# Smaller pieces of the residual and gate loads, more load buffers and another product order in a mixture-of-experts block

## The chip, the cores and the metric

The kernel runs on one core of one Trainium2 chip. The metric is the device time of one launch in microseconds (us), the median of several runs. The engines are TensorE (PE in the rows; its weight loads are PEld), VectorE (DVE), ScalarE (ACT), GpSimd (POOL) and SyncE (SP). SyncE here only issues DMA transfers.

## The reference, cut to what matters

One layer of a transformer block over 256 tokens of width 2048: an attention and pooling part, then a feed-forward part with 16384 experts, of which every token picks 128 (8 heads, 16 each) with a gate. All of it is float32.

```python
mod = silu(c) @ ada_w + ada_b                      # 6 vectors of 2048
shift1, scale1, gate1, shift2, scale2, gate2 = split(mod, 6)
...                                                # attention and pooling part gives h
xn2 = rms_norm(h, norm2_g) * (1 + scale2) + shift2
# peer_ffn: router scores, top 16 of 16 x 16 candidates a head, softmax gates
a   = gelu(xn2 . w_down[expert]) * gate            # for the 128 chosen experts of a token
out = sum over the chosen experts of a * w_up[expert]
h   = h + gate2 * out
return rms_norm(h, final_g)
```

## The kernel before

**The order of the work.** The kernel is a list of steps that run one after the other. A step is one block of weights of 128 x 2048 float32 (1 MB), read as two halves of 128 x 1024 (0.5 MB), and the matmuls on it. The list holds the first projections, attention with its output, the router's queries, and then the expert part, which is computed densely for the first 192 tokens (`ND`): every one of the 128 blocks of 128 experts is multiplied with all 192 tokens, and a gate that is zero for experts not chosen is multiplied in between. The last 64 tokens (`SP`) are done sparsely: their chosen rows are gathered from memory and worked on by VectorE (`sparse_step`, 128 gathers of 1 MB, spread over the steps; 0.95, 0.47, 0.42 and 0.55 a step in the four stages below, the first of them from its step 24 on).

The expert part has four stages of 64 steps (`HB`): half 0 down, half 0 up, half 1 down, half 1 up. Both halves and both products are in `steps`; `n0` is the first down step of a half where the loop over `half` uses it, and after that loop it is the first down step of half 1. The text below counts the steps of each stage from 0.

**A step's matmuls.** In half 0 the down step is `exact`: float32 matmuls straight from the load buffer (`L353`, 16 products, each of which the trace shows as two matmuls). In the other steps each half of a block is split: ScalarE casts it to a rounded part `hi` (`L166`), VectorE subtracts that and leaves the rest `lo` (`L172`). There are 4 buffers of each (`HL_BUFS`). In half 1 down `pair` multiplies `hi` with both parts of the tokens (384 columns, `L189`) and `lo` with the rounded part (192 columns, `L190`). In the up steps the token side is stationary, and it is split too: `prep` casts on ScalarE (`L1114`) and subtracts twice on VectorE (`L1116`). The results stay in all 8 banks of PSUM for the 64 steps: bank `2q+t` holds column quarter `q` (512 columns) of token group `t`. Tokens 0 to 127 (`t = 0`) have a rounded and a rest part of 128 columns each (H and L below); tokens 128 to 191 (`t = 1`) have both parts side by side in one stationary operand of 128 columns (X), and `fold` adds the two halves of the result at the end. With `wh` and `wl` for the two parts of the weights a quarter needs H wh, L wh, H wl, X wh, X wl: five matmuls, twenty a step. A step calls `mm` twice (`part` 0 and 1), each for two quarters, that is, for one half of the block.

The order inside a part is all products with `hi` and then all with `lo`. In the last step of all the order is another (`last`): the eight X products first, `hi` and `lo` by turns.

**Loads.** `want` puts all loads of the kernel in one list in the order of their use. `fill` issues them on SyncE's queue as long as a buffer is free: 5 buffers `raw`, and behind them the list `spare`, which is filled with other memory for some stretches (`room(True)`: three pieces of `hT`, in half 0 up from step 1 to the last 8 steps, and again from step 26 of half 1 down). `take` gets the oldest load, `give` returns its buffer and calls `fill`. In half 0 down, steps 0 to 19 also carry the last 20 of the 32 halves of the modulation matrix for `gate2` (`ada_half`): VectorE multiplies the load with `cb` and sums it (`L219`), so one load in three waits for VectorE there. In the same steps VectorE runs the router's selection (`route`), in the order of the program.

**The three things around it.**
- `load_gates(q)` brings the gates of half 1 back from memory (`g2d`, written by half 0) into the tile that will take the activations: tiles 0 and 1 in half 0 up, tile 2 at step 0 of half 1 down, a small tile 3 at step 24. A tile is one transfer of 2 MB on SyncE's queue.
- At step 1 of half 1 down one transfer of 2 MB on SyncE's queue brings `hT` (the block's input, parked in `hsp`) back.
- `residual`, a generator that moves on twice a step, begins after step 4 of half 1 down: it finishes `gate2` on GpSimd (`ada_fix`), stores it as a row, loads it broadcast to all partitions (`g2b`), both on GpSimd's queue, which also issues the gathers; after four turns of rest it transposes `hT` on TensorE, four blocks at a time, and VectorE multiplies half 0's result with `g2b` and adds the transposed block (`L1231`, `L1232`), eight times.

`tick` is one function that a step may carry; it is called behind the step's matmuls, its row work and its side work.

Of the kernel before, what the change touches and what calls it, by code (L numbers as in the profile page):

```python
# [93 lines left out]
def peer_block_kernel(ctx: ExitStack, tc, xT_d, c_d, cols_d, const_d, ada_d, gates_d, wide_d, blk_d, mix_d, br_d,  # L94
# [151 lines left out]
    class Step:  # L246
        def __init__(self, src, mm, evac=None, w=D, ada=(), before=(), after=(), tick=None, exact=False):
            self.exact = exact
            self.src, self.mm, self.evac, self.w = src, mm, evac, w
            self.ada, self.before, self.after, self.tick = list(ada), list(before), list(after), tick  # L250
            self.hs, self.ls = [], []
            self.rows = 0
# [48 lines left out]
    def run():  # L301
# [11 lines left out]
        for n, parts in plan():  # L313
# [18 lines left out]
            if s:  # L332
                side_step(1)
                if s.tick:
                    s.tick()
# [467 lines left out]
    steps[w0 + 2].tick = lambda: table(AF.Sqrt)  # L803
# [211 lines left out]
    def load_gates(q):  # L1015

        a = get_A(half_state[1], q)
        nc.sync.dma_start(a, g2d[:, :, q * AB:q * AB + a.shape[2], :])
# [73 lines left out]

    def open_late():
# [10 lines left out]
    def up_step(half, bl, oc):  # L1104
# [15 lines left out]
        def mm(h_, l_, part):  # L1120
# [6 lines left out]
            def go(q, t, low):  # L1127
# [5 lines left out]
                else:  # L1133
                    nc.tensor.matmul(o, a[:, :P], w, start=st_, stop=sp_)  # L1134
                    if not low:
                        nc.tensor.matmul(o, a[:, P + 2 * SP:], w, start=False, stop=False)  # L1136
# [3 lines left out]
            else:  # L1140
                order = [(q, t, low) for low in (False, True) for q in (2 * part, 2 * part + 1) for t in range(2)]
# [72 lines left out]
    def residual():  # L1214

# [3 lines left out]
        g2b = fin["g2b"] = per.tile([P, D], F32, tag="cb", name="g2b")  # L1219
        nc.gpsimd.dma_start(g2b, row.rearrange("k p -> (k p)").unsqueeze(0).to_broadcast([P, D]))  # L1220
        for _ in range(4):
            yield
# [14 lines left out]
    for half in range(2):  # L1237
# [4 lines left out]
        if half == 0:  # L1242
            for m in range(2 * KC):
                steps[n0 - 12 + m].ada.append((80 + m // 2, m % 2))
            steps[n0 + 2].tick = open_late

            steps[n0 + 5].tick = lambda: side.append(gate_groups())
        oc = []
        for bl in range(HB):
            steps.append(up_step(half, bl, oc))  # L1250
            if half == 0 and bl % AB == 1 and bl > AB:
                steps[-1].tick = lambda q=bl // AB - 1: load_gates(q)
        if half == 0:
            steps[-1].evac = lambda oc=oc: keep(oc)
    steps[n0].tick = lambda: load_gates(NA - 2)
    steps[n0 + 24].tick = lambda: load_gates(NA - 1)
# [8 lines left out]
    def room(on):  # L1265

        spare.clear()
        if on:
            f = hT.rearrange("p k s -> p (k s)")
            spare.extend(f[:, i * HW:(i + 1) * HW] for i in range(KC * ND // HW))  # L1270

    steps[n0 - HB + 1].tick = lambda: room(True)
# [100 lines left out]
```

## Time and profile before

| | |
|---|---|
| median of 3 runs | 2090.99 us (2086.14 to 2091.57) |
| the profiled execution | 2092.7 us, its span 2090.8 us |
| TensorE, its weight loads | 95% and 88% of the span busy |
| VectorE, ScalarE, GpSimd | 80%, 43%, 18% |
| DMA | 648.81 MB, mean 310 GB/s |
| half 0 down, half 0 up | about 732 to 1130 us, 1130 to 1431 us |
| half 1 down, half 1 up | about 1432 to 1763 us, 1763 to 2062 us |

The span is the time from the first to the last instruction of the profiled execution. A matmul counts as busy until its modelled end, and neighbours overlap, so a rate is read from the count of matmuls in a stretch, not from the mean of one. Times in the rows are us from the start of the span unless a column says ns. In waits, "A <- B: total, times, longest" means that A's engine stood idle until B.

### The profile page before, as it was taken

How to read it: one execution, taken by the hardware profiler on the slowest of the kernel's cores; microseconds unless marked ns; L12 is line 12 of the kernel's file. 1: busy time of each engine (PE TensorE's matmuls, PEld its weight loads, DVE VectorE, ACT ScalarE, POOL GpSimd, SP SyncE). 2: the span in 40 equal slices, each digit the busy share in tenths (PEclk: the TensorE clock that was granted, in tenths of full speed). 3: DMA queues.
4: the chain of work that ended last, by engine and by line, in shares of the span. 5: the costliest groups of instructions: out<-in, count | busy, mean ns of one | idle time of the engine just before them, and what ended most of it. 6: DMA issues, size and time to landing. Idle time of an engine off the chain costs nothing.

```text
span 2090.8 us, 33335 instructions
## 1 busy us (share of the span) xinstructions
PE 1986.3 (95%) x12444; PEld 1836.5 (88%) x12444; DVE 1682.5 (80%) x2908; ACT 904.2 (43%) x1473; POOL 378.7 (18%) x384
## 2 busy tenths in 40 slices
PE   6899999999999998999999999998789999999994
PEld 5788999999999998899998888887689999888883
DVE  8987788889888976478886888876678888888886
ACT  3344554544545511012213554544355555545553
POOL 2201231112115700011111010011111112222220
PEclk8999999999999999999999999999799999999997
DMA  9997877788997777699999999989779998999992
GB/s 368 384 342 255 309 266 263 262 286 304 315 327 245 247 244 243 228 355 373 351 353 367 371 330 359 359 333 323 227 264 332 341 334 316 365 348 354 348 349 75
DMA packets 171971, 648.81 MB, mean 310 GB/s; under 512 B 21025, under 2 KB 30529, under 8 KB 155041
## 3 DMA queue, kind: packets, MB, share of 16 engines
q1 hardware_dynamic: 147568, 499.18, 67.3%
q0 software_dynamic: 19200, 136.87, 17.8%
q10 hardware_dynamic: 5042, 10.64, 1.3%
q8 instruction: 98, 1.61, 0.3%
q14 instruction: 63, 0.52, 0.1%
HBM read 636.13 MB, written 10.49 MB: 309 GB/s over the span
## 4 chain that ended last, share of the span: by engine, by line
PE 65%; DMA 12%; DVE 8%; issue 3%; ACT 2%; POOL 0%; DVEq 0%; ACTq 0%; SPq 0%; POOLq 0%
PE oc L1134 11%; PE oc L1132 11%; PE blk L353 10%; PE blk L189 7%; PE oc L1136 6%; DMA raw<-in_ada_dram 4%; PE blk L183 4%; PE blk L184 4%; PE blk L182 4%; PE blk L190 3%; DVE lo L172 2%; DMA raw<-in_wout_dram 2%; DVE raw L219 2%; PE gps L1051 2%; DMA raw<-in_down_dram 2%
## 5 line engine op out<-in xcount | busy, mean ns | idle before, releaser
L172 DVE TENSOR_TENSOR lo<-raw,hi 128x1024 fp32r<-128x1024 f32 (+1 forms) x484 | 575.0, 1196 | 126.1 <-ACT hi L166 122.6
L166 ACT CAST hi<-raw 128x1024 fp32r<-128x1024 f32 (+1 forms) x484 | 491.2, 1021 | 414.6 <-PE oc L1132 128.6
L353 PE MATMUL blk<-hT,raw 128*128 128x192 f32 x2048 | 344.3, 329 | 12.9 <-DMA raw<-in_down_dram 12.9
L353 PEld LDWEIGHTS blk<-hT,raw 128*128 128x128 f32 x2048 | 335.1, 192 | 16.7 <-issue 11.8
L189 PE MATMUL blk<-xn,hi 128*128 128x384 f32 x1024 | 300.0, 365 | 9.5 <-ACT hi L166 8.9
L190 PE MATMUL blk<-xn,lo 128*128 128x192 f32 x1024 | 260.1, 254 | 18.0 <-DVE lo L172 17.9
L219 DVE SCALAR_TENSOR_TENSOR raw<-raw,cb 128x1024 f32<-128x1024 f32 x165 | 213.5, 1312 | 45.9 <-DMA raw<-in_ada_dram 45.3
L1169 POOL DMA_INDIRECT rows<-in_up_dram,spidx x64 | 126.7, 1979 | 512.5 <-DVE rows L1187 253.7
L190 PEld LDWEIGHTS blk<-xn,lo 128*128 128x128 f32 x1024 | 198.9, 194 | 20.7 <-DVE lo L172 20.7
L189 PEld LDWEIGHTS blk<-xn,hi 128*128 128x128 f32 x1024 | 195.6, 191 | 10.8 <-ACT hi L166 9.5
L1132 PE MATMUL oc<-hi,a 128*128 128x512 f32 x512 | 202.6, 396 | 1.7 <-ACT hsum L1085 1.7
L1134 PE MATMUL oc<-hi,a 128*128 128x512 f32 x512 | 202.7, 396 | 0.0
L1134 PE MATMUL oc<-lo,a 128*128 128x512 f32 x512 | 202.5, 396 | 0.0
L1132 PE MATMUL oc<-lo,a 128*128 128x512 f32 x512 | 202.5, 396 | 0.0
L1136 PE MATMUL oc<-hi,a 128*128 128x512 f32 x512 | 202.5, 395 | 0.0
L166 ACT CAST hi<-hT 128x1024 fp32r<-128x1024 f32 x118 | 124.1, 1052 | 122.9 <-PE oc L1132 72.1
L172 DVE TENSOR_TENSOR lo<-hT,hi 128x1024 fp32r<-128x1024 f32 x118 | 142.8, 1223 | 33.6 <-ACT hi L166 30.7
L1180 DVE SCALAR_TENSOR_TENSOR rows<-rows,rows 128x2048 f32<-128x2048 f32 x64 | 146.2, 2284 | 27.9 <-DMA rows<-in_rows_dram,spidx 27.8
L1169 POOL DMA_INDIRECT rows<-in_rows_dram,spidx x64 | 62.7, 980 | 561.5 <-DVE a L1116 233.6
L1187 DVE SCALAR_TENSOR_TENSOR rows<-rows,sph,rows 128x2048 f32<-128x2048 f32 x63 | 147.8, 2345 | 0.8 <-DMA rows<-in_up_dram,spidx 0.8
L182 PE MATMUL blk<-xna,hi 128*128 128x256 f32 x480 | 139.3, 290 | 0.0
L184 PE MATMUL blk<-xna,lo 128*128 128x256 f32 x480 | 136.3, 284 | 0.0
(298 smaller groups left out, 3990.7 us busy)
## 6 DMA issues: line engine op xcount, KB each, us to landing
raw<-in_down_dram SPq DMA_DIRECT2D x229, 512.0 KB, 6.7
raw<-in_ada_dram SPq DMA_DIRECT2D x165, 512.0 KB, 5.7
raw<-in_up_dram SPq DMA_DIRECT2D x165, 512.0 KB, 6.9
hT<-in_up_dram SPq DMA_DIRECT2D x91, 512.0 KB, 7.2
raw<-in_blk_dram SPq DMA_DIRECT2D x80, 512.0 KB, 5.8
raw<-in_wout_dram SPq DMA_DIRECT2D x32, 512.0 KB, 6.1
raw<-in_wq_dram SPq DMA_DIRECT2D x32, 512.0 KB, 5.6
xraw<-in_ada_dram SPq DMA_DIRECT2D x27, 512.0 KB, 6.4
```

What stands on the lines that cost most here:

```text
L166: nc.scalar.copy(hi, r)
L172: nc.vector.tensor_sub(lo, r, s.hs[i].bitcast(F32))
L182: nc.tensor.matmul(out, wh, ah, start=start, stop=False)
L184: nc.tensor.matmul(out, wl, ah, start=False, stop=stop)
L189: nc.tensor.matmul(ps[:, :2 * ND], wh, a.rearrange("p s n -> p (s n)"), start=start, stop=False)
L190: nc.tensor.matmul(ps[:, :ND], wl, a[:, 0, :], start=False, stop=stop)
L219: nc.vector.scalar_tensor_tensor(raw, raw, 1.0, cb[:, i * HW:(i + 1) * HW], op0=ALU.mult, op1=ALU.mult, accum_out=modp[:, i, m:m + 1])
L353: nc.tensor.matmul(st["ps"][:, :ND], raw[:, c], a, start=k == 0, stop=k == KC - 1)
L1132: nc.tensor.matmul(o, a[:, P:P + 2 * SP], w, start=st_, stop=sp_)
L1134: nc.tensor.matmul(o, a[:, :P], w, start=st_, stop=sp_)
L1136: nc.tensor.matmul(o, a[:, P + 2 * SP:], w, start=False, stop=False)
L1169: nc.gpsimd.indirect_dma_start(rows[:, j % 2, :], None, table_rows["down" if j < NP else "up"], bass.IndirectOffsetOnAxis(sp["idx"][:, j % ...
```

## The change

It has these parts:
- a step carries a list `ticks` in place of one `tick`;
- `load_gates(n, q, parts)` brings a tile in four transfers, one after each of four steps from `n` on: tiles 0 and 1 from the same steps as before, tile 2 from step 18 of half 1 down, and tile 3 whole at step 24 as before;
- `room("split")`: from step 1 of half 0 down to its step 56 the four `hi` buffers are spare load buffers;
- `gate_row`: the row of `gate2` is finished and loaded after step 22 of half 0 down;
- `hT` comes back in four transfers, after steps 2, 4, 6 and 8 of half 1 down, and `residual` begins after step 10, with one turn of rest;
- the order of the up products: by quarter and token group, `hi` and `lo` by turns, H wh, H wl, L wh, X wh, X wl.

```diff
--- before.py
+++ after.py
@@ -244,12 +244,12 @@
 
 
     class Step:
-        def __init__(self, src, mm, evac=None, w=D, ada=(), before=(), after=(), tick=None, exact=False):
+        def __init__(self, src, mm, evac=None, w=D, ada=(), before=(), after=(), exact=False):
             self.exact = exact
             self.src, self.mm, self.evac, self.w = src, mm, evac, w
-            self.ada, self.before, self.after, self.tick = list(ada), list(before), list(after), tick
+            self.ada, self.before, self.after = list(ada), list(before), list(after)
             self.hs, self.ls = [], []
-            self.rows = 0
+            self.rows, self.ticks = 0, []
 
     steps = []
     side, side2, score_q = deque(), deque(), []
@@ -331,8 +331,8 @@
                 sparse_step()
             if s:
                 side_step(1)
-                if s.tick:
-                    s.tick()
+                for f in s.ticks:
+                    f()
             for a in parts[1]:
                 act(a)
         if steps[-1].evac:
@@ -800,7 +800,7 @@
         while len(order) - len(todo) < seen * len(order) // total:
             t.ada.append(todo.popleft())
 
-    steps[w0 + 2].tick = lambda: table(AF.Sqrt)
+    steps[w0 + 2].ticks.append(lambda: table(AF.Sqrt))
 
     def fix_mods():
         ada_fix(32, 48)
@@ -1012,10 +1012,15 @@
                 hs["A"].append(tail.rearrange("p (g n u) -> p g n u", n=n, u=TG))
         return hs["A"][q]
 
-    def load_gates(q):
-
-        a = get_A(half_state[1], q)
-        nc.sync.dma_start(a, g2d[:, :, q * AB:q * AB + a.shape[2], :])
+    def load_gates(n, q, parts=4):
+
+        def load(g):
+            a = get_A(half_state[1], q)
+            nc.sync.dma_start(a[:, g], g2d[:, g, q * AB:q * AB + a.shape[2], :])
+
+        for i in range(parts):
+            g = slice(i * NG // parts, (i + 1) * NG // parts)
+            steps[n + i].ticks.append(lambda g=g: load(g))
 
     def gate_groups():
         hs = half_state[0]
@@ -1090,6 +1095,15 @@
             nc.scalar.activation(dst, ps[:, :ND].rearrange("p (g u) -> p g u", u=TG), AF.Gelu)
         hs["evac"] = bl + 1
 
+    def room(where=None):
+
+        spare.clear()
+        if where == "h":
+            f = hT.rearrange("p k s -> p (k s)")
+            spare.extend(f[:, i * HW:(i + 1) * HW] for i in range(KC * ND // HW))
+        elif where:
+            spare.extend(wst.tile([P, HW], F32, tag="hi", bufs=HL_BUFS, name="spare") for _ in range(HL_BUFS))
+
     def open_late():
         pa_ctx.close()
         pp["pk"] = ext(tc.tile_pool(name="pk", bufs=1))
@@ -1131,14 +1145,14 @@
                 if t:
                     nc.tensor.matmul(o, a[:, P:P + 2 * SP], w, start=st_, stop=sp_)
                 else:
-                    nc.tensor.matmul(o, a[:, :P], w, start=st_, stop=sp_)
-                    if not low:
-                        nc.tensor.matmul(o, a[:, P + 2 * SP:], w, start=False, stop=False)
+                    nc.tensor.matmul(o, a[:, :P], w, start=st_, stop=False)
+                    if low:
+                        nc.tensor.matmul(o, a[:, P + 2 * SP:], h_[q // 2][:, c], start=False, stop=sp_)
 
             if last:
                 order = [(q, t, low) for t in (1, 0) for q in range(4) for low in (False, True)]
             else:
-                order = [(q, t, low) for low in (False, True) for q in (2 * part, 2 * part + 1) for t in range(2)]
+                order = [(q, t, low) for q in (2 * part, 2 * part + 1) for t in range(2) for low in (False, True)]
             for o in order:
                 go(*o)
 
@@ -1211,15 +1225,17 @@
             evacuate(fin["acc"][:, 0, c], oc[2 * q], q)
             fold(fin["acc"][:SP, 1, c], oc[2 * q + 1])
 
-    def residual():
-
+    def gate_row():
         ada_fix(80, 96)
         row = gdram.tile([KC, P], F32, name="g2row")
         nc.gpsimd.dma_start(row.rearrange("k p -> p k"), mod[:, 80:96])
-        g2b = fin["g2b"] = per.tile([P, D], F32, tag="cb", name="g2b")
-        nc.gpsimd.dma_start(g2b, row.rearrange("k p -> (k p)").unsqueeze(0).to_broadcast([P, D]))
-        for _ in range(4):
-            yield
+        fin["g2b"] = per.tile([P, D], F32, tag="cb", name="g2b")
+        nc.gpsimd.dma_start(fin["g2b"], row.rearrange("k p -> (k p)").unsqueeze(0).to_broadcast([P, D]))
+
+    def residual():
+
+        g2b = fin["g2b"]
+        yield
         for t in range(2):
             for q in range(4):
                 acc = fin["acc"][:, t, q * 512:(q + 1) * 512]
@@ -1242,18 +1258,20 @@
         if half == 0:
             for m in range(2 * KC):
                 steps[n0 - 12 + m].ada.append((80 + m // 2, m % 2))
-            steps[n0 + 2].tick = open_late
-
-            steps[n0 + 5].tick = lambda: side.append(gate_groups())
+            steps[n0 + 1].ticks.append(lambda: room("split"))
+            steps[n0 + 2].ticks.append(open_late)
+            steps[n0 + 5].ticks.append(lambda: side.append(gate_groups()))
+            steps[n0 + 22].ticks.append(gate_row)
+            steps[n0 + HB - 8].ticks.append(lambda: room())
         oc = []
         for bl in range(HB):
             steps.append(up_step(half, bl, oc))
-            if half == 0 and bl % AB == 1 and bl > AB:
-                steps[-1].tick = lambda q=bl // AB - 1: load_gates(q)
         if half == 0:
             steps[-1].evac = lambda oc=oc: keep(oc)
-    steps[n0].tick = lambda: load_gates(NA - 2)
-    steps[n0 + 24].tick = lambda: load_gates(NA - 1)
+    for q in range(NA - 2):
+        load_gates(n0 - HB + AB * (q + 1) + 1, q)
+    load_gates(n0 + 18, NA - 2)
+    load_gates(n0 + 24, NA - 1, 1)
 
 
     share = [0.95] * (HB - RS) + [0.47] * HB + [0.42] * HB + [0.55] * (HB - 4)
@@ -1262,18 +1280,12 @@
         n = int(seen / total * 2 * NP + 1e-6)
         seen += w
         steps[n0 - 2 * HB + RS + i].rows = int(seen / total * 2 * NP + 1e-6) - n
-    def room(on):
-
-        spare.clear()
-        if on:
-            f = hT.rearrange("p k s -> p (k s)")
-            spare.extend(f[:, i * HW:(i + 1) * HW] for i in range(KC * ND // HW))
-
-    steps[n0 - HB + 1].tick = lambda: room(True)
-    steps[n0 - 8].tick = lambda: room(False)
-    steps[n0 + 26].tick = lambda: room(True)
-    steps[n0 + 1].tick = lambda: nc.sync.dma_start(hT, hsp)
-    steps[n0 + 4].tick = lambda: side.append(residual())
+    steps[n0 - HB + 1].ticks.append(lambda: room("h"))
+    steps[n0 - 8].ticks.append(lambda: room())
+    steps[n0 + 26].ticks.append(lambda: room("h"))
+    for q in range(4):
+        steps[n0 + 2 + 2 * q].ticks.append(lambda c=slice(4 * q, 4 * q + 4): nc.sync.dma_start(hT[:, c, :], hsp[:, c, :]))
+    steps[n0 + 10].ticks.append(lambda: side.append(residual()))
     run()
```

## Rows read from the trace of the kernel before

**Rows 1.** The page's first part: busy us (share of the span) and instructions.
```profile
PE 1986.3 (95%) x12444; PEld 1836.5 (88%) x12444; DVE 1682.5 (80%) x2908; ACT 904.2 (43%) x1473; POOL 378.7 (18%) x384
```

**Rows 2.** Stretches: us, busy of PE, PEld, DVE, ACT, POOL; PE clock, DMA share, GB/s.
```profile
732.00:860.00 128.00, 115.11 (x675) 111.21 (x674) 83.55 (x359) 16.05 (x35) 1.14 (x2) 0.97 0.72 237
860.00:895.00 35.00, 35.00 (x219) 34.98 (x218) 12.93 (x38) 3.71 (x14) 2.02 (x2) 1.00 0.77 268
895.00:1130.00 235.00, 234.59 (x1563) 234.43 (x1563) 186.82 (x475) 51.14 (x240) 37.25 (x37) 1.00 0.97 357
...
1450.00:1470.00 20.00, 13.45 (x79) 12.56 (x78) 9.66 (x12) 7.54 (x13) 2.31 (x2) 0.83 0.84 333
...
1480.00:1502.00 22.00, 8.06 (x41) 7.43 (x40) 6.71 (x10) 4.77 (x7) 1.57 (x2) 0.61 0.77 213
...
1519.00:1550.00 31.00, 25.45 (x154) 23.94 (x154) 24.54 (x30) 16.73 (x26) 2.39 (x2) 0.89 0.69 234
...
1600.00:1612.00 12.00, 11.23 (x77) 10.72 (x77) 9.56 (x12) 7.33 (x11) 1.68 (x1) 1.00 1.02 387
1612.00:1700.00 88.00, 88.00 (x620) 88.00 (x620) 75.97 (x87) 51.32 (x79) 13.52 (x8) 1.00 0.93 341
```

**Rows 3.** Waits of TensorE, 732 to 900 us: total, times, longest.
```profile
PE blk L353 <- DMA raw<-in_down_dram: 12.9, 12, 2.3
```

**Rows 4.** Waits of SyncE's queue, 732 to 860 us.
```profile
SPq L141 <- DVE raw L219: 41.8, 8, 6.7
SPq L141 <- DVE ge L965: 24.1, 4, 7.2
```

**Rows 5.** Waits of TensorE, 1430 to 1612 us.
```profile
PE blk L190 <- DVE lo L172: 17.9, 8, 12.2
```

**Rows 6.** Waits of VectorE, 1437 to 1550 us.
```profile
DVE acc L1231 <- DMA g2b<-g2row: 17.0, 1, 17.0
```

**Rows 7.** DMA issues by line: count, KB each, median us to landing.
```profile
raw<-in_down_dram SPq DMA_DIRECT2D x229, 512.0 KB, 6.7
...
A<-g2d SPq DMA_DIRECT2D x3, 2016.0 KB, 15.0
...
hT<-hsp SPq DMA_DIRECT2D x1, 2048.0 KB, 14.5
...
g2row<-mod POOLq DMA_DIRECT2D x1, 8.0 KB, 14.2
```

**Rows 8.** The first gather on GpSimd, in order of time: start, us.
```profile
883.16 1.06 POOL L1169 DMA_INDIRECT rows<-in_rows_dram,spidx  x1 [131.95 <-DVE spidx L1162]
```

**Rows 9.** VectorE by line, 1502 to 1550 us: count, busy, mean ns.
```profile
L1232 DVE TENSOR_TENSOR acc<-acc,hpt 64x512 f32<-64x512 f32 (+1 forms) x6 | 4.1, 682 | 0.6
L1231 DVE TENSOR_TENSOR acc<-acc,g2b 64x512 f32<-64x512 f32 (+1 forms) x6 | 4.1, 679 | 0.0
```

**Rows 10.** TensorE in order of time, last up step, its first eight matmuls.
```profile
2057.55 0.40 PE L1132 MATMUL oc<-hi,a 128*128 128x512 f32 x1
...
2059.18 0.40 PE L1132 MATMUL oc<-lo,a 128*128 128x512 f32 x1
```

**Rows 11.** TensorE in order of time, wide stage: ten matmuls, first and last.
```profile
173.26 0.39 PE L182 MATMUL acc<-hi,xnb 128*128 128x512 f32 x1
...
175.30 0.39 PE L182 MATMUL acc<-hi,xnb 128*128 128x512 f32 x1
```

**Rows 12.** VectorE and ScalarE by line, half 1 up, 1800 to 2000 us.
```profile
L172 DVE TENSOR_TENSOR lo<-raw,hi 128x1024 fp32r<-128x1024 f32 x53 | 63.8, 1221 | 18.8 <-ACT hi L166 17.4 <-ACT a L1114 1.4
L1187 DVE SCALAR_TENSOR_TENSOR rows<-rows,sph,rows 128x2048 f32<-128x2048 f32 x25 | 58.6, 2346 | 0.0
...
L1116 DVE TENSOR_TENSOR a<-A,a 128x128 fp32r<-128x128 f32 x86 | 18.1, 251 | 0.0
...
L166 ACT CAST hi<-raw 128x1024 fp32r<-128x1024 f32 x53 | 55.8, 1054 | 59.9 <-PE oc L1132 47.1 <-DVE lo L172 12.8
```

**Rows 13.** Waits of TensorE over the whole span.
```profile
PE oc L1132 <- ACT hsum L1085: 1.7, 1, 1.7
```

## Prediction

> **What bounds the kernel now.** I read the page's busy line first, then the span cut into stretches, then who waits for whom in the bad stretches, then DMA issues, then single instructions. TensorE is busy 95% of the span [rows 1], so only two things can shorten it: stretches where it is not at full rate, and its rate.
>
> The stretches [rows 2] give the first. In 860 to 895 us, half 0's exact down products, TensorE retires 219 matmuls in 35 us: 0.160 us each, with no idle time. In 732 to 860, the same loop, it retires 675 in 128 us; at 0.160 these need 107.9, so **20.1 us are lost**. Half 1's down products run at full rate in 1612 to 1700: 620 in 88 us, 0.142 each. Against that, 79 matmuls in 1450 to 1470 lose 20 − 11.2 = **8.8**; 41 in 1480 to 1502 lose 22 − 5.8 = **16.2**; 154 in 1519 to 1550 lose 31 − 21.9 = **9.1**; 77 in 1600 to 1612 lose **1.1**. The clock column shows 0.61 to 0.97 in these stretches, so matmuls at the lower of the two levels are in the sums.
>
> Who is late? In the first stretch TensorE waits for down blocks still in transit [rows 3], and the SyncE queue that issues them stands behind VectorE: it reloads buffers in order, one load in three is a row of the modulation matrix which VectorE consumes, and VectorE sits in the router meanwhile, 7.2 us at the longest [rows 4]. In half 1 TensorE waits for the split halves [rows 5]. In 1450 to 1470 the blocks are late, behind two transfers of 2 MB that take 15.0 and 14.5 us (a 512 KB load takes 6.7) [rows 7]. In 1480 to 1502 VectorE stands 17.0 us in `residual`'s first multiplication, waiting for the broadcast gate row [rows 6], whose first half alone, the column-to-row store, takes 14.2 us to land [rows 7]; the next `lo` stands behind it. In 1519 to 1550 VectorE is overbooked with residual work.
>
> **The change, part by part.**
>
> *Four more load buffers in half 0's down stage* (`room("split")`). The `hi` buffers are idle there, as exact steps split nothing. While the modulation halves run (steps 0 to 19), a step takes three loads: with 5 buffers a freed one is wanted again after 5/3 × 5.1 = 8.5 us (a step is 32 × 0.160 = 5.1), 6.7 of it transit [rows 7], so 1.8 are left for a late VectorE. With 9 it is 15.3 − 6.7 = 8.6, above the longest hold of 7.2. The rate needed is 3 × 0.524 MB / 5.1 us = 308 GB/s; 357 and 387 are seen [rows 2]. So nearly all of 20.1 goes; I leave 1.5 for the first steps. Bounds: 0 and 8 left (holds that follow each other). **−18.6.** The spares must be free before the next stage splits: they are withdrawn at step 56, and nine loads last 4.5 steps.
>
> *The gate row earlier* (step 22 of half 0 in place of step 4 of half 1): two POOL additions, a store, a broadcast of 1 MB. POOL then waits about 14 us between store and broadcast; before, gathers were queued behind that, now nothing: the first gather issues at 883.16 after POOL has been idle 131.95 us [rows 8]. POOL is not tied to step 22 either: it goes when the last modulation half is reduced, about step 20, 732 + 20 × 5.1 = 834 us in the new run, and is free by 848; the first gathers come after step 24, about 860. Without that margin of some 12 us the first gather, then VectorE, then the one-hot products would be late by what lacks. The 16.2 us vanish. Next late there would be `hT`, which lands long before. **−16.2**, bounds −16.2 and −10.
>
> *`hT` in four pieces at steps 2, 4, 6, 8, half 1's third gate tile in four at steps 18 to 21 (before: whole, at steps 1 and 0).* The same bytes, now passing the down loads on SyncE's queue 0.5 MB at a time. With `hT`, a two-step period moves four loads, 0.84 gathered rows of 1 MB and one piece: about 3.5 MB in 9.1 us, 385 GB/s, just what 1600 to 1612 shows (387). I leave 1.5 of the 8.8 (bounds 0 and 4): **−7.3**. In steps 18 to 21 a step asks for two loads, 0.42 rows and one piece, 2.0 MB in 4.55 us = 440 GB/s, more than any stretch shows: at 385 such a step takes 5.2 us, and 0.65 × 4 = 2.6, partly covered by the five buffers: **+1.5** (0 to 3). In half 0's up stage the tiles come the same way but with eight buffers: 0. The 1.1 us at 1600 (the last, small gate tile) stay.
>
> *Residual later* (first work in step 11, not 5). Same VectorE work: two operations of 0.68 us a step [rows 9], for 8 steps. VectorE has 88 − 75.97 = 12 us spare in 19.3 steps [rows 2], 0.62 a step; so it falls 1.36 − 0.62 = 0.74 behind a step, 5.9 in all. Before, it entered this already late; now it has its lead over TensorE (at most two steps, 9.1 us). I leave 4.5 of the 9.1 (bounds 0 and 9.1): **−4.6**.
>
> *The order of up products.* Twenty matmuls a step as before, now H·wh, H·wl, L·wh, X·wh, X·wl for each column quarter, in place of all wh, then all wl (H, L: the rounded part and rest of tokens 0 to 127; X: both of the other 64). Does a repeated stationary side run faster? The trace has a direct answer: the last step already runs X eight times in a row, and its eight matmuls start 1.63 us apart from first to last, 0.233 each [rows 10], the up stage's rate, each with its own weight load. Price **0**. A gain isn't excluded: in the wide stage, where one of three repeats, nine intervals take 2.04 us, 0.227 each [rows 11]; at that rate 2560 matmuls save 6.3 ns each, 16 us. The nearer row is that of the same products: 0. The Trainium skill ("TensorE: Matmul & The Clock Gate", Step-by-step) says that the load is a separate instruction so that one can load once and multiply repeatedly, and gives 216 ns from one matmul of 512 columns to the next; as an estimate, 8 repeats in 20 at that pace would save 8 × 17 ns × 128 steps = 17 us. No row here shows that rate, and the last step speaks against it.
>
> What the order does change is when the halves are needed. In a part of ten matmuls, `hi` was free after the sixth and `lo` wanted at the seventh; now `hi` is free after the ninth and `lo` wanted at the second. Four buffers are two steps, 40 matmuls, so from a free `hi` to the wanted `lo` there were 40 × 0.233 = 9.3 us and are now 32 × 0.233 = 7.5. In it must go a cast of 1.05, the subtraction of 1.22 and what VectorE has ahead of it: a row of 2.35, two subtractions of 0.25, the other half's 1.22 [rows 12]: 6.3. It fits with 1.2 to spare; today TensorE waits 1.7 us once in these stages [rows 13], at the entry, where the first `lo` comes one subtraction after `hi`. **+1.5** (0 to 5).
>
> **Sum.** −18.6 − 16.2 − 7.3 + 1.5 − 4.6 + 0 + 1.5 = −43.7. The profiled execution took 2092.7 (span 2090.8, the rest around it unchanged): 2049.0. It lies 1.7 above the median of 2090.99, so for a median: **2047**. With every bound at its best the sum is −54.2, 2037 (the rate left out); with every one at its worst −18.9, 2072.
>
> **Rivals.**
> *The matmul rate rises.* For it: 0.227 in the wide stage. Against it: the eight repeats at 0.233. 2047 − 16 = 2031. The rule of the Trainium skill above speaks for this case too.
> *The transfers take part back.* Half 0's holds chain (+6.5), the residual stays as costly (+4.5), `hT` and gate pieces delay blocks (+2.5 and +1.5): 2047 + 15 = 2062. For it: 0.97 of the DMA engines' time in 895 to 1130. Against it: TensorE has no idle time there.
> *The row's move only shifts its wait*: POOL is held when the first gathers are due; of 14 us of hold 10 would reach TensorE: 2057. Against it: the idle 132 us.
> *Slower*: the split falls behind in the up stages. Nothing else in a step grows, so it is decided by the 1.2 us to spare: when VectorE's queue ahead of a subtraction grows past it by 0.34 us on each of 128 steps, all 43.7 are gone; at 0.45 a step the time is 2105. For it: VectorE is already 86% busy in the down stage beside it (75.97 of 88) [rows 2]. Against it: a late part delays the rows and casts with it, so a lag doesn't add up by itself.
>
> **Chances.** Forecast 0.72 (own range 2037 to 2057), rate 0.08, transfers 0.12, shifted wait 0.03, slower 0.05. Of the last a part ends within 0.3% (6 us, about what a measurement can tell here): faster 0.94, same 0.02, slower 0.04. The range of 8 in 10 takes the forecast's and the transfers' case and the middle of the rate's: 2030 to 2065.
>
> **What the new profile would show.** Right: no wait for in_down in half 0 beyond some 2 us and over 290 GB/s there; no wait for `g2b` on VectorE; full clock from 1390 to 1510; up matmuls still 0.233 apart with as many weight loads as matmuls; small new waits of oc for `lo`. Wrong: up intervals under 0.228, waits for `lo` spread over the up steps, or a gap ahead of the first one-hot product.

## The result and the profile after

The changed kernel takes **2042.2 us** (median of 4 runs, 2038.8 to 2045.6), the kernel before 2091.3 in the same comparison: a ratio of 0.977, with an interval of 0.974 to 0.979. 2047 was forecast, in a range of 2030 to 2065. The profiled execution took 2038.8 us, with a span of 2036.6.

The page's first part, beside [rows 1]: TensorE has lost 12 us of modelled busy time and 54 us of span.

```profile
PE 1974.8 (97%) x12444; PEld 1830.6 (90%) x12444; DVE 1682.9 (83%) x2908; ACT 904.9 (44%) x1473; POOL 380.6 (19%) x384
```

The stretches, with the columns of [rows 2]:

```profile
730.00:858.00 128.00, 128.00 (x793) 127.78 (x793) 94.17 (x394) 17.35 (x39) 3.33 (x6) 1.00 0.89 295
858.00:893.00 35.00, 35.00 (x228) 34.98 (x227) 21.09 (x50) 6.96 (x32) 6.15 (x6) 1.00 0.98 371
...
1429.00:1449.00 20.00, 20.00 (x143) 20.00 (x142) 17.77 (x21) 11.65 (x19) 3.35 (x2) 1.00 1.00 396
...
1459.00:1481.00 22.00, 22.00 (x160) 22.00 (x160) 20.75 (x26) 12.80 (x19) 1.78 (x2) 1.00 0.91 325
1481.00:1498.00 17.00, 17.00 (x124) 17.00 (x123) 16.29 (x23) 9.17 (x15) 3.36 (x2) 1.00 0.77 278
1498.00:1529.00 31.00, 30.84 (x215) 30.59 (x214) 26.92 (x32) 16.98 (x27) 5.04 (x3) 1.00 0.99 361
1529.00:1600.00 71.00, 70.25 (x485) 69.99 (x484) 59.45 (x70) 41.26 (x64) 10.06 (x6) 1.00 0.97 360
```

Half 0's down products start at 730.1 us here. In their first 128 us TensorE retires 793 matmuls, where [rows 2] had 675, at 295 GB/s in place of 237; the wait for blocks of [rows 3] is gone. In half 1 the stretches with the `hT` pieces (1429 to 1449), the residual (1459 to 1498) and the gate pieces (1498 to 1529) run at 0.137 to 0.144 us a matmul and at full clock (beside the residual the count holds its transposes, which are shorter); the first of them moves 396 GB/s, and that without loss. All that TensorE waits for in the blocks of the expert part is in four rows of its waits:

```profile
PE blk L189 <- ACT acc L551: 1.4, 1, 1.4
PE oc L1146 <- ACT hsum L1090: 1.4, 1, 1.4
...
PE blk L190 <- DVE lo L172: 0.9, 2, 0.7
...
PE oc L1148 <- DVE lo L172: 0.2, 1, 0.2
```

GpSimd in order of time (start, us, and in brackets how long it stood and for whom): the gate row's sum at 830, its store at 831, the broadcast at 845, and 16 us later the first gather.

```profile
830.25 0.22 POOL L226 TENSOR_TENSOR mod<-modp 128x16 f32<-128x16 f32 x1 [82.35 <-DVE spare L219]
...
831.06 1.21 POOL L1231 DMA_DIRECT2D g2row<-mod  x1 [0.29 <-POOL mod L227]
844.71 0.55 POOL L1233 DMA_DIRECT2D g2b<-g2row  x1 [12.45 <-DMA g2row<-mod]
861.05 1.03 POOL L1183 DMA_INDIRECT rows<-in_rows_dram,spidx  x1 [15.79 <-DVE spidx L1176]
```

During the store TensorE lost nothing. This is the same view of stretches:

```profile
831.00:845.00 14.00, 14.00 (x88) 14.00 (x87) 13.34 (x41) 0.66 (x2) 1.49 (x2) 1.00 0.89 151
```

88 matmuls at 0.160 us are 14.1 us. But the 16 DMA engines are busy 89% of that time for 151 GB/s, which matters below.

An up step in order of time, one quarter and the start of the next: H wh, H wl, L wh, X wh, X wl.

```profile
1200.99 0.40 PE L1146 MATMUL oc<-hi,a 128*128 128x512 f32 x1
1201.22 0.40 PE L1146 MATMUL oc<-lo,a 128*128 128x512 f32 x1
1201.45 0.40 PE L1148 MATMUL oc<-hi,a 128*128 128x512 f32 x1
1201.69 0.40 PE L1148 MATMUL oc<-lo,a 128*128 128x512 f32 x1
1201.92 0.40 PE L1150 MATMUL oc<-hi,a 128*128 128x512 f32 x1
1202.15 0.40 PE L1146 MATMUL oc<-hi,a 128*128 128x512 f32 x1
```

Starts are 0.23 to 0.24 us apart whether the stationary side (`a`) repeats or not.

By stage, from the first to the last start of a stage's first product, and the ratio to the kernel before of the same comparison:

| kernel | half 0 down, us | half 1 down, us | median, us | ratio (interval) |
|---|---|---|---|---|
| before | 397.6 | 331.2 | 2091.3 | |
| changed | 377.4 | 299.9 | 2042.2 | 0.977 (0.974 to 0.979) |
| order_alone | 392.8 | 330.5 | 2091.6 | 1.000 (0.999 to 1.001) |
| buffers_alone | 377.4 | 331.0 | 2075.5 | 0.993 (0.992 to 0.995) |
| gate_row_alone | 400.3 | 318.9 | 2081.6 | 0.995 (0.994 to 0.997) |
| pieces_alone | 394.9 | 313.8 | 2075.0 | 0.993 (0.990 to 0.996) |
| all_but_order | 377.3 | 301.8 | 2045.6 | 0.976 (0.974 to 0.978) |
| two_spares | 380.9 | 303.3 | 2046.8 | 0.975 (0.972 to 0.978) |
| whole_again | 377.3 | 311.5 | 2049.4 | 0.977 (0.975 to 0.980) |
| late_row | 377.3 | 320.3 | 2060.5 | 0.983 (0.981 to 0.986) |
| store_again | 377.2 | 309.0 | 2047.6 | 0.978 (0.975 to 0.981) |
| more_vector_new | 377.5 | 298.9 | 2042.2 | 0.975 (0.972 to 0.977) |
| more_vector_old | 377.3 | 300.7 | 2043.9 | 0.976 (0.974 to 0.978) |
| wide_tile | 377.2 | 302.8 | 2047.1 (one run) | |

The kernel before had medians of 2091 to 2096 in the five comparisons, so few of the last eight can be told apart by the whole time: intervals are 4 to 6 thousandths wide, 8 to 12 us. The stages are from one execution of each. Ahead of half 0 down, where no kernel differs, these executions take 729.3 to 735.8 us, so a stage says more than the whole. Where a stage has the same work and no wait it repeats within 0.3 us (nine kernels with four spare buffers: 377.2 to 377.5); half 1 down of the changed kernel, without an edit of its own, spreads over 298.9 to 303.3. With stalls in it the spread can be wider: pieces_alone and late_row have the same code in that stage and take 313.8 and 320.3.

### The profile page after: what moved, and what is told of

It reads as the page before. It is cut to its first block, busy times and chain, and to the rows that moved or that the text cites. A ratio compares the mean times of both kernels' runs of the same rounds, so it can differ in the third digit from the quotient of the medians.

```text
span 2036.6 us, 33368 instructions
## 1 busy us (share of the span) xinstructions
PE 1974.8 (97%) x12444; PEld 1830.6 (90%) x12444; DVE 1682.9 (83%) x2908; ACT 904.9 (44%) x1473; POOL 380.6 (19%) x384
## 4 chain that ended last, share of the span: by engine, by line
PE 73%; DVE 7%; DMA 6%; ACT 2%; issue 2%; POOL 0%; DVEq 0%; ACTq 0%; POOLq 0%
PE blk L353 16%; PE oc L1146 12%; PE oc L1148 12%; PE blk L189 8%; PE oc L1150 6%; PE blk L183 4%; PE blk L182 4%; PE blk L184 4%; PE blk L190 3%; DVE lo L172 2%; DMA raw<-in_wout_dram 2%; PE gps L1056 2%; DMA raw<-in_blk_dram 2%; ACT hi L166 1%; DVE raw L219 1%
## 5 line engine op out<-in xcount | busy, mean ns | idle before, releaser
L1183 POOL DMA_INDIRECT rows<-in_up_dram,spidx x64 | 133.6, 2087 | 491.3 <-DVE rows L1201 438.1
L353 PE MATMUL blk<-hT,raw 128*128 128x192 f32 x1280 | 212.3, 326 | 0.0
L353 PEld LDWEIGHTS blk<-hT,raw 128*128 128x128 f32 x1280 | 207.7, 190 | 0.0
L219 DVE SCALAR_TENSOR_TENSOR raw<-raw,cb 128x1024 f32<-128x1024 f32 x153 | 198.0, 1314 | 9.8 <-DMA raw<-in_ada_dram 9.8
```

Of the source, the lines that this page charges most:

```text
L219: nc.vector.scalar_tensor_tensor(raw, raw, 1.0, cb[:, i * HW:(i + 1) * HW], op0=ALU.mult, op1=ALU.mult, accum_out=modp[:, i, m:m + 1])
L353: nc.tensor.matmul(st["ps"][:, :ND], raw[:, c], a, start=k == 0, stop=k == KC - 1)
L1183: nc.gpsimd.indirect_dma_start(rows[:, j % 2, :], None, table_rows["down" if j < NP else "up"], bass.IndirectOffsetOnAxis(sp["idx"][:, j % ...
```

## The experiments

### The order alone, and all but the order

order_alone is the kernel before with these two edits; all_but_order is the changed kernel without them.

```diff
-                    nc.tensor.matmul(o, a[:, :P], w, start=st_, stop=sp_)
-                    if not low:
-                        nc.tensor.matmul(o, a[:, P + 2 * SP:], w, start=False, stop=False)
+                    nc.tensor.matmul(o, a[:, :P], w, start=st_, stop=False)
+                    if low:
+                        nc.tensor.matmul(o, a[:, P + 2 * SP:], h_[q // 2][:, c], start=False, stop=sp_)
...
-                order = [(q, t, low) for low in (False, True) for q in (2 * part, 2 * part + 1) for t in range(2)]
+                order = [(q, t, low) for q in (2 * part, 2 * part + 1) for t in range(2) for low in (False, True)]
```

> The kernel before with nothing but the new order of the up products. Forecast's theory: a repeated stationary side is loaded again and saves nothing, so the up intervals stay at 0.233 us; the halves are wanted earlier, which costs 0 to 1.5 us: 0.999 to 1.001 of the time before. Rival (repeats shorten the interval, as 0.227 in the wide stage would have it): up intervals under 0.228 us, about 16 us less, 0.992. Rival (the split falls behind): waits of TensorE for lo in many up steps, more than 1.003.

> The changed kernel with the old order of the up products. Theory, after the order alone gave no difference: the order is worth nothing here either, 0.976 to 0.978 of the time before, the same as with it, and the up intervals stay at 0.233 us. Rival (the order pays only once the rest no longer waits): this kernel is slower than the changed one by 8 us or more, 0.981. Rival (the order costs): faster by some us, 0.974, and the small waits of oc for lo in the last up steps are gone.

The order alone gives 1.000 (0.999 to 1.001). Its stretches show the rate:

```profile
1180.00:1300.00 120.00, 120.00 (x516) 96.62 (x515) 96.22 (x128) 60.85 (x77) 11.09 (x12) 1.00 0.94 348
```

516 matmuls in 120 us, 0.2326 each, with 515 weight loads beside them. The kernel before has 516 in the same stretch too. And TensorE's waits in the up products, now with one for `lo`:

```profile
PE oc L1132 <- ACT hsum L1085: 0.4, 1, 0.4
...
PE oc L1134 <- DVE lo L172: 0.2, 1, 0.2
```

Without the order the changed kernel takes the same time within the intervals, and half 1 down is 301.8 us. Both rivals fall: repeats don't make the products faster, with or without the other waits, and of the earlier need of `lo` TensorE's waits show 0.2 us.

### The four buffers alone, and two in place of four

buffers_alone adds to the kernel before what the diff has of `room("split")` and `room()` in half 0. two_spares is the changed kernel with

```diff
-            spare.extend(wst.tile([P, HW], F32, tag="hi", bufs=HL_BUFS, name="spare") for _ in range(HL_BUFS))
+            spare.extend(wst.tile([P, HW], F32, tag="hi", bufs=HL_BUFS, name="spare") for _ in range(HL_BUFS // 2))
```

> The kernel before with nothing but the four idle hi buffers as spare load buffers in half 0 down. Theory: the 20 us lost between 732 and 860 us go, 18 to 20 us less, 0.990 to 0.991, and nothing else moves. Rival (the loads get faster but the first gathers or the products of one-hots come late instead): at most half of it, 0.995 or more, with a new gap of TensorE near the first gather.

> The changed kernel with two spare load buffers in half 0 down in place of four. By the count of the forecast, seven buffers give 7/3 x 5.1 = 11.9 us, less 6.7 of transit 5.2 us for a late VectorE, whose holds were up to 7.2: a few of the stretch's 20 lost us come back, 2 to 6, 0.978 to 0.980. Rival (any spare will do, the stage was short of one load in flight): nothing comes back. Rival (transit grows with every load in flight): half comes back, 10 us, 0.981.

The buffers take half 0 down from 397.6 to 377.4 us, 20.2 less, and half 1 down stays (331.0). The median falls by 15.7, where 18 to 20 were expected; the profiled execution (2068.8) is the fastest of its four, and where the slower ones lost is in no trace. With two spares the stage takes 380.9; the whole, 0.975, doesn't show it. The size, 3.5, is in the expected 2 to 6, but not its reason: TensorE waits for a block once in the stage, 3.1 us, and that falls into 840 to 850, when the gate row is stored:

```profile
840.00:850.00 10.00, 6.86 (x42) 6.56 (x41) 8.81 (x28) 0.33 (x1) 0.00 (x0) 1.00 1.15 120
```

42 matmuls in 10 us, DMA at 120 GB/s with its engines full. (The share comes from the packets' times and can pass 1.) The holds by VectorE, for which the count was made, cost nothing with seven buffers. The rival that any spare will do holds but for the store.

### The gate row alone, the pieces alone

gate_row_alone is the kernel before with `gate_row` as in the diff, called after step 22; the residual still begins after step 4 with its four turns of rest, the transfers are whole. pieces_alone has the pieces of `hT` and gates and the residual after step 10, and stores and loads the gate row when the residual begins.

> The kernel before with nothing but the gate row finished and loaded after step 22 of half 0 down. Theory: VectorE's wait of 17 us for the row goes, and TensorE's 16 us with it. If the 9 us lost beside the residual were a late effect of that wait, they go too: 25 us less, 0.988. If they are VectorE's own overload, 16 us less, 0.992. The 9 us behind the two whole transfers stay in both. Rival (the wait only moves to the first gathers): under 8 us gained, and a wait of VectorE for the first gather longer than before.

> The kernel before with nothing but the transfers in pieces and the residual begun after step 10; the gate row is still finished and loaded when the residual begins, four turns ahead of its use. Theory: the 9 us behind the whole transfers go, while VectorE's wait for the row comes back some six steps later with nearly its old 16 us of TensorE time: 7 to 9 us less, 0.996. Rival (the later start is itself what hides the row): 20 us less or more, 0.990. Rival (the pieces only spread the delay): 0 to 3 us, 0.999 or more.

The row alone makes half 1 down 12.3 us shorter and the median 9.6, less than either size expected (16 or 25). VectorE's wait for the row is gone. What is left is in two stretches:

```profile
1452.00:1470.00 18.00, 12.38 (x69) 11.48 (x68) 8.35 (x11) 6.29 (x10) 1.11 (x1) 0.83 0.90 365
...
1500.00:1530.00 30.00, 24.37 (x150) 23.14 (x150) 22.44 (x27) 13.93 (x22) 2.29 (x2) 0.92 0.69 234
```

At 0.142 us a matmul 8.2 us are lost behind the whole transfers and 8.7 beside the residual. In the second VectorE is busy for only 22.44 of 30 us, so its time isn't what lacks. Split where the residual's last four turns begin, it shows where the loss lies:

```profile
1479.00:1505.00 26.00, 25.82 (x187) 25.57 (x185) 22.65 (x30) 9.50 (x16) 2.28 (x2) 1.00 0.80 286
1505.00:1530.00 25.00, 19.37 (x114) 18.14 (x114) 17.57 (x22) 13.59 (x21) 1.15 (x2) 0.91 0.66 218
```

VectorE's two operations are in all eight turns. In the last four ScalarE also copies the other 64 partitions (`nc.scalar.copy(acc[SP:], pt[SP:])`), which waits for VectorE's addition into the same tile. The next casts stand behind that copy, and VectorE and TensorE wait for the casts (waits of ScalarE, VectorE, TensorE; the last line is ScalarE in the changed kernel, 1459 to 1505 us, where nothing is lost):

```profile
ACT acc L1237 <- DVE acc L1235: 14.2, 4, 4.7
DVE lo L172 <- ACT hi L166: 6.9, 4, 1.7
PE blk L189 <- ACT hi L166: 3.6, 2, 2.4
...
ACT acc L1250 <- DVE acc L1248: 3.0, 3, 1.0
```

No run changed the copy, so how much of the 8.7 hangs on it is not shown.

Half 0 down, 400.3, is 2.7 above the longest of the others with five buffers (392.8 to 397.6). The store falls there now, at 857 us: in its 14 us and the 14 after it TensorE retires 78 and 74 matmuls, 3.7 us less than full rate, and waits for blocks for 2.7.

The pieces with the later residual make it 17.4 us shorter, against an expected 7 to 9; the rival that the later start is what hides the row put it at 20 or more. VectorE's wait for the row, which was to come back with nearly its old size, is in its waits:

```profile
DVE acc L1245 <- DMA g2b<-g2row: 2.9, 1, 2.9
```

2.9 us, where [rows 6] had 17.0. The store and the broadcast take about as long as ever; but before, GpSimd had stood behind a gather whose row VectorE had reached late. These are GpSimd's gather and store, two lines of the kernel before and two of pieces_alone:

```profile
1467.58 1.68 POOL L1169 DMA_INDIRECT rows<-in_up_dram,spidx  x1 [19.00 <-DVE rows L1187]
1470.52 1.25 POOL L1218 DMA_DIRECT2D g2row<-mod  x1 [0.29 <-POOL mod L227]
...
1477.21 1.68 POOL L1183 DMA_INDIRECT rows<-in_up_dram,spidx  x1 [11.97 <-DVE rows L1201]
1480.16 1.25 POOL L1232 DMA_DIRECT2D g2row<-mod  x1 [0.29 <-POOL mod L227]
```

By the count of its matmuls step 5 of the kernel before begins at about 1456 us, and the store goes 14 us later; in pieces_alone it goes when step 11 begins, at 1480. Whether the pieces did that or the later start, no run tells, as pieces_alone has both. The price of the row didn't go with the wait, either: half 1 down is still 13.9 above the changed kernel's, and it is lost behind the store:

```profile
1480.00:1494.00 14.00, 14.00 (x102) 14.00 (x101) 7.87 (x9) 4.32 (x7) 1.67 (x2) 1.00 1.01 200
1494.00:1506.00 12.00, 7.48 (x49) 6.73 (x49) 6.47 (x9) 5.55 (x9) 1.14 (x2) 1.00 0.96 366
```

### The whole transfers and the late row, each put back

whole_again is the changed kernel with `load_gates(n0, NA - 2, 1)` and one transfer of `hT` after step 1. late_row is the changed kernel with the row stored and loaded when the residual begins:

```diff
-            steps[n0 + 22].ticks.append(gate_row)
...
-        g2b = fin["g2b"]
-        yield
+        gate_row()
+        g2b = fin["g2b"]
+        for _ in range(4):
+            yield
```

> The changed kernel with hT and the third gate tile whole again at their old places (steps 1 and 0 of half 1 down); gate row, buffers, order and the residual after step 10 as changed. Theory: the 9 us in the first steps of half 1 down come back and no more, 0.980 to 0.981, and the residual's steps still cost nothing, as VectorE has five steps to get its lead back. Rival (the residual's former 9 us were an after-effect of that stretch, whenever the residual begins): 15 us or more come back, 0.984. Rival (whole transfers were harmful only together with the late gate row): nothing comes back.

> The changed kernel with the gate row finished and loaded only when the residual begins (step 11 of half 1 down), with four turns of rest as before; everything else as changed. Theory now, after the pieces alone left VectorE a wait of 2.9 us for the row: most of the old 17 us was an effect of the whole transfers, which held a gathered row, the gather behind it and so GpSimd's row store; without them the late row costs 3 to 8 us, 0.979 to 0.981. Rival (the forecast's term as it stood): 16 us, 0.985.

whole_again: half 1 down is 311.5, 11.6 more than changed (8 to 13 by the spread of the others). By the whole time, 0.977 against an expected 0.980 to 0.981, it can't be told from the changed kernel: its median is 3.7 us above that of all_but_order in the same comparison. In the stage the loss is in the first steps, and next to none beside the residual, where 283 matmuls in 40 us are 0.141 each:

```profile
1429.00:1449.00 20.00, 14.15 (x74) 13.27 (x74) 10.62 (x13) 8.50 (x14) 1.68 (x1) 0.75 0.87 339
1462.00:1502.00 40.00, 39.48 (x283) 39.23 (x282) 34.55 (x43) 20.39 (x33) 5.03 (x3) 1.00 0.81 291
```

So the 9 us beside the residual aren't a fixed after-effect of the early stall: five steps later VectorE has its lead back.

late_row: half 1 down is 320.3, **20.4 more**, and the whole 0.983. The stage's code is that of pieces_alone, which is 13.9 above the changed kernel, so the row's price here is 14 to 20 us, known no better from one execution each. Yet VectorE waits for the row for only 6.2 us:

```profile
DVE acc L1249 <- DMA g2b<-g2row: 6.2, 1, 6.2
```

The rival's size is about right, and its cause is a part at most. The stretches and the DMA of the store's time (its busy share and GB/s in 40 slices, and the down loads issued in it) show another:

```profile
1462.50:1476.50 14.00, 12.30 (x88) 12.06 (x86) 7.68 (x9) 4.44 (x8) 1.25 (x1) 1.00 1.06 195
1476.50:1490.00 13.50, 9.11 (x41) 8.46 (x42) 6.17 (x9) 4.68 (x9) 1.56 (x2) 0.75 0.92 331
1490.00:1530.00 40.00, 36.09 (x232) 35.09 (x231) 33.91 (x43) 17.28 (x27) 3.46 (x3) 0.91 0.82 274
```

```profile
DMA  9699999999989999999996976442999996979638
GB/s 211 140 293 269 281 304 410 421 398 398 398 363 456 386 365 378 290 238 141 105 130 94 94 24 35 36 47 35 176 118 105 105 70 82 70 94 105 70 12 35
DMA packets 645, 2.72 MB, mean 195 GB/s; under 512 B 113, under 2 KB 113, under 8 KB 516
...
raw<-in_down_dram SPq DMA_DIRECT2D x4, 512.0 KB, 13.9
```

The store moves 8 KB, 16 values for each of 128 partitions, and each value goes to a place of its own, 4 bytes. While it runs the DMA engines are full and the rest flows at 195 GB/s, in the second half at under 110 for most slices; at its full rate the stage moves 341 [rows 2]. Down loads issued then take 13.9 us to land, where [rows 7] has 6.7. TensorE still has blocks then (88 matmuls), runs dry in the next 13.5 us (41, at a granted clock of 0.75), and the residual meets a VectorE without lead. The kernel before has the same stretch behind its own store, which the reading of [rows 6] as VectorE's wait alone leaves out:

```profile
1470.50:1484.70 14.20, 12.68 (x92) 12.44 (x90) 7.57 (x9) 4.48 (x8) 1.25 (x1) 1.00 1.04 189
```

### The store by itself

store_again is the changed kernel with a second store of the same 8 KB when the residual begins. Nobody reads it.

```diff
         g2b = fin["g2b"]
+        again = gdram.tile([KC, P], F32, name="again")
+        nc.gpsimd.dma_start(again.rearrange("k p -> p k"), mod[:, 80:96])
         yield
```

> The changed kernel with a second, unused copy of the gate row's store (8 KB in pieces of 4 bytes) issued when the residual begins; nobody reads it and nobody waits for it. Theory: the store itself holds the DMA engines for some 14 us (in late_row they are full at 195 GB/s then, where the stage asks for 330), the five load buffers run dry and the residual's VectorE lead is spent, so half 1 down is 8 to 16 us longer, 0.980 to 0.985. Rival (the late row's price is VectorE's wait for it): no change, 0.976 to 0.978.

Half 1 down is 309.0, 9.1 more than changed and 5.7 more than the longest of those without an edit there:

```profile
1458.00:1472.00 14.00, 14.00 (x102) 14.00 (x101) 10.63 (x13) 5.57 (x9) 3.42 (x3) 1.00 1.06 184
1472.00:1482.00 10.00, 6.83 (x45) 6.08 (x44) 5.41 (x7) 4.01 (x6) 0.00 (x0) 1.00 0.88 305
1482.00:1520.00 38.00, 35.81 (x245) 34.14 (x244) 35.70 (x45) 21.70 (x35) 5.03 (x3) 1.00 0.83 293
```

184 GB/s for 14 us, then 45 matmuls in 10 us (3.6 lost), then 245 in 38 us (3.2 lost), without any wait of VectorE for a transfer of the row. By the whole time, 0.978, it can't be told from the changed kernel; by the stage and its stretches it can. So of the 13.9 to 20.4 us of the late row some 6 to 10 are the store's load on the DMA engines, by one execution of each; what is left goes with the broadcast, the wait of 6.2 us and what follows them, and those weren't taken apart further.

### More work for VectorE

Both kernels have the changed kernel's everything, more_vector_old with the old order, and in every fourth up step

```diff
             st["a"] = a
+            if bl % 4 == 2:
+                t = x2["rows"]
+                nc.vector.tensor_scalar(t, t, 1.0, 0.0, op0=ALU.mult, op1=ALU.add)
```

> The changed kernel with one more VectorE operation in every fourth up step (the gathered rows' tile times 1 plus 0, 128 x 2048, 32 times in all), which uses up the room in VectorE's queue. By the forecast's count 6.3 us of work plus this one (1.1 to 2.4 us) must fit into 7.5 us with the new order: if it takes over 1.2 us, TensorE waits for lo in most of these 32 steps, up to 1.1 us each, 10 to 35 us more, 0.982 to 0.993. Rival (the count of the window is too strict, since the casts run ahead and a delay isn't repeated): 0 to 5 us more, 0.977 to 0.979.

> The same additional VectorE operations with the old order of the up products, whose window is 9.3 us: 0 to 3 us more than the changed kernel by the forecast's count, 0.976 to 0.978; so if the new order's earlier lo has a price under load, it is the difference of these two kernels. Rival (no window at all, VectorE's time alone counts): the same time as with the new order.

The additional operation is in VectorE's lines with its count, busy time and mean:

```profile
L1135 DVE TENSOR_SCALAR rows<-rows 128x2048 f32<-128x2048 f32 x32 | 39.4, 1232 | 0.0
```

39.4 us more for VectorE, and no time: 2042.2 and 2043.9, the new order not behind the old. At 1.23 us it brings the counted work to 7.5, just the window's length, so it isn't a hard test of the count; it does show that no price lies near.

### What sets 0.233?

wide_tile is the changed kernel with `[P, 512]` for the tile of the split tokens and two such tiles in place of three.

> A look at what sets the up products' 0.233 us: the changed kernel with the split tokens of an up step in a tile of 512 columns in place of 384, so that each tile begins at a multiple of 2 KB, and two such tiles in place of three. If the place of the stationary operand sets the interval, it falls towards 0.227 us (16 us less in all); if not it stays at 0.233 us. Two tiles leave one step less of lead, so waits of oc may appear.

```profile
1180.00:1300.00 120.00, 120.00 (x516) 96.64 (x515) 97.08 (x126) 57.62 (x77) 11.25 (x12) 1.00 0.95 345
```

Again 516 in 120 us. The tile's width and place, as far as this run moves them, aren't it. Why the wide stage has 0.227 [rows 11] stays open.

## Why the prediction was right, step by step

- **Half 0's buffers**, forecast −18.6: −20.2 in the stage. TensorE has no wait left there. The SyncE count (5/3, 9/3 of a step) gave the right sign; by the same count seven buffers leave 5.2 us for holds of 7.2, too little, and two_spares has no wait that such a hold explains.
- **The gate row's way past the gathers**: right nearly to the microsecond. It was forecast to go at 834 and be free at 848, with the first gather at 860; it went at 831, was free at 845, and the gather came at 861. What the text did not see is that the place has a second merit: a store that fills the DMA engines falls where nine buffers are full.
- **Half 1's sum**, forecast −16.2 − 7.3 + 1.5 − 4.6 = −26.6: measured −31.3. The row's term stands about where it was put: 12.3 alone, and 13.9 or 20.4 by the two kernels that lack only the early row in this stage (pieces_alone, late_row). Its mechanism was a part of it, as the store's load on the DMA engines isn't in the text. Mis-sized are the pieces and the later residual together: −10.4 forecast, −17.4 alone and −19.0 from gate_row_alone to the changed kernel. Of these the whole transfers, put back, take 11.6; some 6 to 7 are left for the later start, which wasn't run by itself.
- **The residual**, forecast to keep 4.5 of 9.1: keeps next to nothing (160 + 124 matmuls in the 39 us from 1459, 0.137 each, the shorter transposes among them). That the loss goes when the residual meets a VectorE with its lead fits: in late_row and pieces_alone the lead is spent, and it costs again. The reason given for the 9.1 doesn't hold: VectorE, said to be overbooked from 1519 to 1550, is busy for 24.54 of these 31 us [rows 2]. In the changed kernel it is busy for 37.04 of 39, and nothing is lost. By gate_row_alone the loss begins with the turns in which ScalarE's copy waits for VectorE.
- **The pieces**, +1.5 twice: nothing for `hT`, and some 0.5 us for the gate tile (215 matmuls in 31 us). The limit of 385 GB/s was taken from the highest stretch shown; 396 was moved here without a wait. The Trainium skill ("DMA: Bandwidth & Descriptors", Where 436 GB/s comes from) puts the limit of loads from memory at about 358 GB/s for one core, a stack's bandwidth divided by its two cores; 396 and 387 in stretches of 20 and 12 us of this kernel, which runs on one core, are above it, so the measurement decides.
- **The order's rate**, 0: shown by order_alone. The rule of the Trainium skill ("TensorE: Matmul & The Clock Gate", Step-by-step), load once and multiply repeatedly, has no effect on the rate here: each matmul brings its own load, 515 beside 516.
- **The order's earlier `lo`**, +1.5: 0.2 us of wait. The slower rival falls with it.
- **The sum**: −43.7 forecast, −49.1 between the medians, −54.2 between the spans of the two profiled executions. The transfers' rival and the shifted wait did not come. Of the 10.5 us by which the spans exceed the forecast half 1 down holds 4.7, half 0 down 1.6, the two up stages 1.6 (the order's +1.5 wasn't paid), and 2.6 lie ahead of the expert part, where nothing was changed. The changed kernel's profiled execution is the fastest of its four, so that the median came within 5 us of 2047 is better than the terms deserve.

## What to carry to other kernels

The length of a wait isn't its price. VectorE waited 17.0, 2.9 and 6.2 us for the row (before, pieces_alone, late_row), and having the row early was worth 12.3, 13.9 and 20.4; so try each part alone and put it back into the finished kernel, and compare stretches beside waits. The parts tried alone add up to 29.7 us and put back to 32.0, against 31.3 together: within the spread of the stage, so no stall is shown to hide another. When an engine is called overbooked, look at its busy time in that very stretch. A transfer's bytes don't tell its price: 8 KB in pieces of 4 bytes held the DMA engines for some 14 us, so put it where buffers are full. Before ordering matmuls for a stationary side that repeats, look for a place where the trace has it repeated.

## What the runs showed of the hardware

- A store of 8 KB in 4-byte pieces took 12.5 to 16.2 us to land in the kernels whose profile gives a landing. The DMA engines were 0.89 to 1.15 busy meanwhile in the rows shown, and moved 120 to 200 GB/s in all; down loads issued beside it took 13.9 us in late_row, where [rows 7] has 6.7. The Trainium skill ("DMA: Bandwidth & Descriptors", Rules for kernel authors) says that a last dimension that isn't contiguous becomes one descriptor per element and should be rearranged. The profile counts packets and not descriptors, so it shows the price of such a store and not that count; and by late_row and store_again the other queues pay too.
- In the up stages float32r products of 512 columns start 0.233 us apart, whether the stationary side repeats two, eight or no times in a row, and in both layouts of its tile that were tried. In the wide stage it is 0.227 [rows 11], which stays open.
